# Second attention: the order k, first q, v; all of q's products in plain fp32; one instruction for a pair's offset

## The chip, the cores and the metric

One core of a Trainium2 chip runs the whole program in one launch. The metric is the device time of one execution in microseconds. TensorE (PE) does matmuls into PSUM; VectorE (DVE), ScalarE (ACT) and GpSimd (POOL) work on SBUF and PSUM; SyncE (SP) issues most DMA loads.

## The reference

Two blocks of a transformer on 256 tokens of width 1024, all in fp32. The first block has two layers, each attention and a convolutional FFN; the second block is a gated delta rule mixer with a mixture of experts. The change is in the second layer's attention:

```python
hk = rmsnorm(x, kv_norm)
k, v = jnp.split(hk @ w_kv_b, 2, axis=-1)            # 4 heads of 64 each
h = rmsnorm(x, attn_norm[l])
q = partial_rope(heads(h @ w_q_b[i], N_HEADS), cos, sin)   # 16 heads of 64
...
logits = jnp.einsum('bkgnqd,bknpd->bkgnqp', qb, kcat) * (HEAD_DIM ** -0.5)
logits = jnp.where(mask, logits, NEG)                # a window of 128
m = jnp.maximum(jnp.max(logits, axis=-1, keepdims=True), sink)
e = jnp.exp(logits - m)
p = e / (jnp.sum(e, axis=-1, keepdims=True) + jnp.exp(sink - m))
out = jnp.einsum('bkgnqp,bknpd->bkgnqd', p, vcat)
x = x + out.reshape(...) @ w_o
```

## The kernel before

Activations lie transposed, features on partitions: `x` is 8 blocks of 128 features by 256 tokens. A projection is done in chunks of 256 output columns: one DMA of 1 MB brings the chunk's weights (`raw`, 3 buffers), and each of the 8 feature blocks gives two products (the chunk's two column halves), each a 128x128 block of weights on 256 tokens, summed in PSUM (`acc`, 4 buffers).

A product comes in two forms. In the plain form the fp32 weights and the fp32 activations (`xf`) go to PE as they are (L262). In the split form both are cut into a high and a low part of type fp32r: ACT copies the high part (`whi`, L204; `xh`, L400), DVE subtracts to get the low one (`wlo`, L207; `xl`, L401), and PE does three matmuls, high by high, low by high, high by low (L217 to L219; in `proj_tm`, which gives v with tokens on partitions, L306 and L314 to L316). An `Act` holds activations with the first `plain` blocks in plain form and the rest split; in the second attention `plain` is 2 of 8, for `act` (k and v), `actq` (q) and `out`. Weights are split in pieces of 512 columns, 5 buffers of each part, so a chunk with 2 plain blocks has 3 pieces.

The second attention (its block begins at L770) goes: activations for k and v, row norms and tables for the rotation, activations for q, k's projection and rotation, v's projection, and then 4 chunks of q. A chunk holds two pairs of heads, each pair in `softmax_pair` and `attend_pair`: the mask is laid into PSUM by a matmul (L445), the scores are added (L447, L449), DVE takes the row maxima (`mm`, L451) and makes the offset `nb` (L457, L458), ACT does the exponentials with their sums (L463) and the sink's (L468), DVE scales (`pr`, L475), PE transposes (L489), DVE and ACT copy the transposed tiles to SBUF, and PE multiplies by v (L497). Then w_o in 4 chunks (first 2 blocks plain) and the FFN's w_up.

There is no order by hand here: the tile framework puts each engine's instructions in an order when the program is built, by readiness and by place in the program, so PE's queue mixes a pair's instructions with products of later chunks. Each engine then works through its own queue in that order. The block at the end of the program, for the experts, has its own scheduling and is not touched.

Of the kernel before, what the change touches and what calls it, by code (L numbers as in the profile page):

```python
# [13 lines left out]
F32 = mybir.dt.float32  # L14
F32R = mybir.dt.float32r
I32 = mybir.dt.int32
AF = mybir.ActivationFunctionType
ALU = mybir.AluOpType
# [3 lines left out]
P = 128  # L22
T = 256
D = 1024
KD = D // P
NH = 16
# [53 lines left out]
def tile_two_blocks(ctx: ExitStack, tc: tile.TileContext, A, out_ap):  # L80
    nc = tc.nc
# [3 lines left out]
    B = SimpleNamespace(few=2, n=0)  # L85
# [35 lines left out]
    x = cp.tile([P, KD, T], F32, name="x")  # L121
# [8 lines left out]
    sk = fp.tile([P, NH], F32, name="sk")  # L130
# [21 lines left out]
    masks = [fp.tile([P, 384], F32R, name=f"maskr{i}") for i in range(2)]  # L152
# [27 lines left out]
    class Act:  # L180


        def __init__(self, plain, n, tag=None, pool=None, bufs=2, sfx=""):
            pool = pool or B.wk
            self.plain = plain
            tags = ("xh", "xl") if tag is None else tag
            self.h = pool.tile([P, n, T], F32R, name="xh", tag=tags[0], bufs=bufs)
            self.l = pool.tile([P, n, T], F32R, name="xl", tag=tags[1], bufs=bufs)
            self.f = plain and pool.tile([P, plain, T], F32, name="xf", tag="xf" + sfx, bufs=bufs)
# [48 lines left out]
    def proj(*args, **kw):  # L238
        for _ in proj_steps(*args, **kw):
            pass  # L240
# [59 lines left out]
    def proj_tm(raw, act, evac, parts=None):  # L300

        pss = [B.pa.tile([P, T], F32, name="acc", tag="acc") for _ in range(2)]
        n = act.plain
        for t in range(2):
            for k in range(n):
                nc.tensor.matmul(pss[t], act.f[:, k, t * P : (t + 1) * P], raw[:, k * 256 : (k + 1) * 256], start=k == 0, stop=False)  # L306
        for a, n1, hi, lo in parts or parts_of(raw[:, n * 256 :], 2048 - n * 256, n * 256):
            hv = hi.rearrange("p (k c) -> p k c", c=256)
            lv = lo.rearrange("p (k c) -> p k c", c=256)
            for t in range(2):  # L310
                s = slice(t * P, (t + 1) * P)
                for k in range(n1 // 256):
                    kg = a // 256 + k
                    nc.tensor.matmul(pss[t], act.h[:, kg, s], hv[:, k, :], start=kg == 0, stop=False)  # L314
                    nc.tensor.matmul(pss[t], act.h[:, kg, s], lv[:, k, :], start=False, stop=False)
                    nc.tensor.matmul(pss[t], act.l[:, kg, s], hv[:, k, :], start=False, stop=kg == KD - 1)  # L316
        for t in range(2):
            evac(t, pss[t])
# [64 lines left out]
    def rstd_of(sums):  # L383
        return rstd_rows(rstd_cols(sums))

    def gained(src, gi):

        act = Act(2, KD)
        for _ in gained_steps(act.h, act.l, src, gi, act.f):
            pass  # L390
        return act

    def gained_steps(hi, lo, src, gi, full=None):
        for k in range(KD):
            g = nv[:, gi, k : k + 1]
            if full is not None and k < 2:
                nc.scalar.activation(full[:, k], src[:, k], AF.Copy, scale=g)
                continue
            h, l = (f(k) if callable(f) else f[:, k] for f in (hi, lo))
            nc.scalar.activation(h, src[:, k], AF.Copy, scale=g)  # L400
            nc.vector.scalar_tensor_tensor(l, src[:, k], g, h.bitcast(F32), op0=ALU.mult, op1=ALU.subtract)  # L401
            if k % 2:
                yield
# [21 lines left out]
    def rope_to(dst, ps, tab):  # L425

        raw = B.wk.tile([P, 2, T], F32, name="qraw", tag="qraw")
        sw = B.wk.tile([P, 2, T], F32, name="qsw", tag="qsw")
        nc.scalar.activation(raw, ps, AF.Copy)
        nc.vector.stream_shuffle(sw, raw, SWAP)  # L430
        nc.vector.tensor_tensor(dst, raw, tab[0], op=ALU.mult)
        nc.vector.tensor_tensor(sw, sw, tab[1], op=ALU.mult)
        nc.vector.tensor_tensor(dst, dst, sw, op=ALU.add)

    def softmax_pair(q, k, mask, sinks):

        cut = ((0, 128), (128, 384))
        mm = B.wk.tile([P, 2, 2], F32, name="mm", tag="mm")
        both = B.pb.tile([P, 2, 512], F32, name="sc", tag="sc", bufs=2)
        sc = [both[:, h, :384] for h in range(2)]  # L440
        hs = [slice(h * HD, (h + 1) * HD) for h in range(2)]

        edges = lambda x: x.rearrange("p (b c) -> p b c", c=P)[:, 0::2] if sinks is None else x
        for s in sc:
            nc.tensor.matmul(edges(s), identr, edges(mask), start=True, stop=False, skip_group_check=True)  # L445
        for s, h in zip(sc, hs):
            nc.tensor.matmul(s[:, 0:128], q[h, 0:128], k[h, 0:128], start=False, stop=True, skip_group_check=True)  # L447
        for s, h in zip(sc, hs):
            nc.tensor.matmul(s[:, 128:384], q[h, 128:256], k[h, :], start=False, stop=True, skip_group_check=True)  # L449
        for i, (a, b) in enumerate(cut):  # L450
            nc.vector.tensor_reduce(mm[:, :, i], both[:, :, a:b], axis=AX.X, op=ALU.max)  # L451
        nb = B.wk.tile([P, 2, 2], F32, name="nb", tag="nb")
        if sinks is None:
            nc.vector.tensor_scalar(nb, mm, -0.125, None, op0=ALU.mult)
        else:
            for h in range(2):
                nc.vector.tensor_scalar(nb[:, h], mm[:, h], 0.125, sinks[h], op0=ALU.mult, op1=ALU.max)  # L457
            nc.vector.tensor_scalar(nb, nb, -1.0, None, op0=ALU.mult)  # L458
        pr = B.wk.tile([P, 2, 384], F32, name="pr", tag="pr")
        sums = B.wk.tile([P, 2, 2], F32, name="sums", tag="sums")  # L460
        for h in range(2):
            for i, (a, b) in enumerate(cut):
                nc.scalar.activation(pr[:, h, a:b], sc[h][:, a:b], AF.Exp, bias=nb[:, h, i : i + 1], scale=0.125,  # L463
                                     accum_out=sums[:, h, i : i + 1])
        if sinks is not None:
            es = B.wk.tile([P, 2, 2], F32, name="es", tag="es")
            for h in range(2):
                nc.scalar.activation(es[:, h], nb[:, h], AF.Exp, bias=sinks[h], scale=1.0)  # L468
            nc.vector.tensor_tensor(sums, sums, es, op=ALU.add)
        rs = B.wk.tile([P, 2, 2], F32, name="rs", tag="rs")  # L470
        nc.vector.reciprocal(rs, sums)
        for h in range(2):
            for i, (a, b) in enumerate(cut):
                if sinks is not None or i:
                    nc.vector.tensor_scalar(pr[:, h, a:b], pr[:, h, a:b], rs[:, h, i : i + 1], None, op0=ALU.mult)  # L475
                else:
                    nc.scalar.activation(pr[:, h, a:b], pr[:, h, a:b], AF.Copy, scale=rs[:, h, i : i + 1])
        return pr, both
# [233 lines left out]
    with phase("ab", 4), tc.tile_pool(name="hp", bufs=1) as hp, weights("ab", 3, 5, 2048, 512):  # L712
# [6 lines left out]
        raw = B.wr.tile([P, 2048], F32, name="raw", tag="raw")  # L719
        for a in range(0, 2048, 512):  # L720
            nc.scalar.dma_start(raw[:, a : a + 512], A["w_v"][0][:, a : a + 512])
        act = Act(2, KD)
        ws = parts_of(raw[:, 512:], 1536, 512)
        both = []
# [14 lines left out]
        for c in range(4):  # L739
# [4 lines left out]
            if c == 1:  # L744
# [3 lines left out]
                y = rstd_cols(sums)  # L748
# [8 lines left out]
        for t in range(8):  # L757
            qk = B.wk.tile([P, 2, T], F32, name="qk", tag="qk")
            proj("w_qk", t, KD, act, None, both=lambda ps: rope_to(qk, ps, tab))
            pr, both = softmax_pair(qk[:, 0, :], qk[:, 1, :], masks[0], None)  # L760
# [7 lines left out]


        act = gained(x, 4)  # L770
        y = rstd_cols(sums)
        tab = tables(y)
        actq = gained(x, 1)
        k1, v1 = (hp.tile([P, 2, 256], F32, name=i, tag=t) for i, t in (("k1", "hh"), ("v1", "hl")))
        proj("w_kv", 0, KD, act, None, both=lambda ps: rope_to(k1, ps, tab))
        raw = B.wr.tile([P, 2048], F32, name="raw", tag="raw")
        nc.sync.dma_start(raw, A["w_kv"][1])
        proj_tm(raw, act, lambda t, ps: nc.scalar.activation(v1[:, t, :], ps, AF.Copy, scale=y[:, t : t + 1]))
        out = Act(2, KD)
        for c in range(4):  # L780
            q1 = B.wk.tile([P, 2, T], F32, name="q1", tag="qk")
            proj("w_q", c, KD, actq, None, both=lambda ps: rope_to(q1, ps, tab))
            for m in range(2):
                t = 2 * c + m
                kvp = t // 4
                heads = [4 * (2 * kvp + s) + t % 4 for s in range(2)]
                pr, both = softmax_pair(q1[:, m, :], k1[:, kvp, :], masks[1], [sk[:, h : h + 1] for h in heads])
                vs = [[v1[:, j, (2 * kvp + s) * HD : (2 * kvp + s + 1) * HD] for j in range(2)] for s in range(2)]
                attend_pair(pr, both, vs[0], vs[1], out, t)
        sums = Sums()  # L790
# [918 lines left out]
```

## Time and profile before

| | |
|---|---|
| time, median of 3 runs | 1313.37 us (1313.19 to 1313.55) |
| the profiled execution: time, span | 1312.89 us, 1311.1 us |
| busy: PE, weight loads, DVE, ACT | 98%, 88%, 78%, 60% |
| k's projection to the last pair's value products | about 324 to 399 us |

The span is the time from the first to the last instruction in the trace, and the rows' times count from its start. PE's matmuls are pipelined: what one costs in a run of them is read from the steps between starts, not from its duration. PEld is the loading of weights, which goes on beside matmuls. A row of the timeline that ends in x8 merges eight records.

### The profile page before, as it was taken

What the parts mean: (1) busy time and instruction counts of PE and PEld (TensorE: products, weight loads), DVE (VectorE), ACT (ScalarE), POOL (GpSimd) and SP (SyncE); (2) the same over time, 40 slices, a digit from 0 to 9 for tenths busy, and PEclk for the clock granted to TensorE, in tenths of its full rate; (3) what the DMA queues carried; (4) which work ended last, traced back from release to release, by engine and by line L of the source; (5) the groups of instructions that cost most, each with busy time, mean ns of one, the idle gap of its engine ahead of it and who ended that gap; (6) DMA issues with size and microseconds to landing.
All of it is one profiled execution on the core that took longest, in us unless ns stands there. A gap on an engine that the chain in (4) does not pass through costs nothing.

```text
span 1311.1 us, 26079 instructions
## 1 busy us (share of the span) xinstructions
PE 1278.9 (98%) x10092; PEld 1149.3 (88%) x10092; DVE 1019.1 (78%) x2215; ACT 790.2 (60%) x1628; POOL 28.5 (2%) x51
## 2 busy tenths in 40 slices
PE   7999999999999999999999999999999999999998
PEld 7888999999879999999888787888987888888877
DVE  6677989866788988755766888666368899999985
ACT  6555667755556677653434464644257887878763
POOL 1000000000000010000100000000000000000000
PEclk9999999999999999999999999999989999999999
DMA  7434555555423555662254323243437999999951
GB/s 285 143 101 139 180 187 176 177 190 177 156 97 130 173 193 184 225 215 79 97 152 126 100 60 102 66 134 99 170 130 288 360 340 354 365 358 376 347 192 35
DMA packets 69570, 244.50 MB, mean 186 GB/s; under 512 B 24128, under 2 KB 26176, under 8 KB 45632
## 3 DMA queue, kind: packets, MB, share of 16 engines
q1 hardware_dynamic: 68288, 241.26, 52.9%
q8 instruction: 81, 1.33, 0.4%
q10 hardware_dynamic: 1152, 1.51, 0.4%
q14 instruction: 49, 0.40, 0.1%
HBM read 240.12 MB, written 2.62 MB: 185 GB/s over the span
## 4 chain that ended last, share of the span: by engine, by line
PE 86%; DVE 9%; ACT 2%; issue 1%; DMA 1%; SPq 0%; DVEq 0%; ACTq 0%
PE acc L217 11%; PE acc L218 11%; PE acc L219 11%; PE acc L292 10%; PE gu L1351 4%; PE gu L1350 4%; PE gu L1352 4%; PE acc L262 4%; PE y L1379 2%; PE y L1380 2%; PE y L1381 2%; PE acc L1614 2%; PE o L1164 2%; DVE wlo L207 1%; PE sc L489 1%
## 5 line engine op out<-in xcount | busy, mean ns | idle before, releaser
L207 DVE TENSOR_TENSOR wlo<-raw,whi 128x512 fp32r<-128x512 f32 (+1 forms) x542 | 467.8, 878 | 102.4 <-ACT whi L204 98.2
L204 ACT ACTIVATE whi<-raw 128x512 fp32r<-128x512 f32 (+1 forms) x542 | 418.1, 780 | 191.9 <-PE acc L218 132.7
L217 PE MATMUL acc<-xh,whi 128*128 128x256 f32 x892 | 258.0, 290 | 0.0
L219 PE MATMUL acc<-xh,wlo 128*128 128x256 f32 x892 | 252.0, 283 | 0.0
L218 PE MATMUL acc<-xl,whi 128*128 128x256 f32 x892 | 251.0, 282 | 0.0
L219 PEld LDWEIGHTS acc<-xh,wlo 128*128 128x128 f32 x892 | 169.8, 190 | 2.5 <-issue 2.5
L217 PEld LDWEIGHTS acc<-xh,whi 128*128 128x128 f32 x892 | 167.7, 188 | 3.0 <-issue 1.5
L218 PEld LDWEIGHTS acc<-xl,whi 128*128 128x128 f32 x892 | 168.0, 188 | 2.5 <-issue 1.5
L292 PE MATMUL acc<-x,raw 128*128 128x256 f32 x640 | 154.0, 386 | 0.4 <-issue 0.4
L292 PEld LDWEIGHTS acc<-x,raw 128*128 128x128 f32 x640 | 116.4, 190 | 15.0 <-issue 0.8
L1351 PE MATMUL gu<-wlo,xgh 128*128 128x512 f32 x256 | 103.7, 405 | 0.0
L1352 PE MATMUL gu<-whi,xgl 128*128 128x512 f32 x256 | 101.0, 394 | 1.7 <-DVE xgl L1307 1.6
L1350 PE MATMUL gu<-whi,xgh 128*128 128x512 f32 x256 | 101.3, 396 | 0.0
L219 PE MATMUL acc<-hh,wlo 128*128 128x256 f32 x352 | 99.6, 283 | 0.0
L218 PE MATMUL acc<-hl,whi 128*128 128x256 f32 x352 | 99.6, 283 | 0.0
L217 PE MATMUL acc<-hh,whi 128*128 128x256 f32 x352 | 99.6, 283 | 0.0
L262 PE MATMUL acc<-xf,raw 128*128 128x256 f32 x296 | 71.3, 379 | 0.0
L217 PEld LDWEIGHTS acc<-hh,whi 128*128 128x128 f32 x352 | 67.6, 192 | 0.0
L219 PEld LDWEIGHTS acc<-hh,wlo 128*128 128x128 f32 x352 | 67.6, 192 | 0.0
L218 PEld LDWEIGHTS acc<-hl,whi 128*128 128x128 f32 x352 | 67.6, 192 | 0.0
L1352 PEld LDWEIGHTS gu<-whi,xgl 128*128 128x128 f32 x256 | 48.6, 190 | 12.2 <-DVE xgl L1307 3.4
L262 PEld LDWEIGHTS acc<-xf,raw 128*128 128x128 f32 x296 | 52.9, 190 | 5.6 <-issue 0.2
(423 smaller groups left out, 2290.4 us busy)
## 6 DMA issues: line engine op xcount, KB each, us to landing
raw<-w_gu SPq DMA_DIRECT2D x64, 1024.0 KB, 7.3
raw<-w_up SPq DMA_DIRECT2D x44, 1024.0 KB, 4.8
raw<-w_ed SPq DMA_DIRECT2D x32, 1024.0 KB, 7.2
raw<-w_gin SPq DMA_DIRECT2D x96, 256.0 KB, 3.3
raw<-w_down SPq DMA_DIRECT2D x16, 1024.0 KB, 4.9
raw<-w_qk SPq DMA_DIRECT2D x8, 1024.0 KB, 5.0
raw<-w_gout SPq DMA_DIRECT2D x32, 256.0 KB, 2.9
raw<-w_down SPq DMA_DIRECT2D x8, 768.0 KB, 4.3
```

The lines of the kernel that those rows point to most:

```text
L204: B.hi = nc.scalar.activation(hi[:, :m], raw[:, a : a + m], AF.Copy)
L207: i = eng.tensor_tensor(lo[:, :m], raw[:, a : a + m], hi[:, :m].bitcast(F32), op=ALU.subtract)
L217: nc.tensor.matmul(ps, wh, ah, start=first, stop=False, skip_group_check=True)
L218: nc.tensor.matmul(ps, wh, al, start=False, stop=False, skip_group_check=True)
L219: return nc.tensor.matmul(ps, wl, ah, start=False, stop=last, skip_group_check=True)
L262: nc.tensor.matmul(ps[:, m], rv[:, k, m * P : (m + 1) * P], full.f[:, k0 + k], start=k0 + k == 0 and m == 0, stop=k0 + k == nk - 1, skip_g ...
L292: nc.tensor.matmul(ps[:, m], raw[:, k, m * P : (m + 1) * P], act(k0 + k), start=k0 + k == 0 and m == 0, stop=k0 + k == nk - 1, skip_group_ ...
L1164: nc.tensor.matmul(o[:, t, h], at[:, d, blk], u[step][:, tu, h], start=i == 0, stop=i == 2)
L1350: nc.tensor.matmul(gu, xgh[:, kg, :], hv[:, k, :], start=kg == 0, stop=False)
L1351: nc.tensor.matmul(gu, xgh[:, kg, :], lv[:, k, :], start=False, stop=False)
L1352: nc.tensor.matmul(gu, xgl[:, kg, :], hv[:, k, :], start=False, stop=kg == KD - 1)
L1379: nc.tensor.matmul(y[g][c], hh[:, j, :], hi[:, s], start=first, stop=False)
```

## The change

Four edits, all in the second attention or in helpers that only it uses that way. q's activations become an `Act` of 8 plain blocks, which then takes one buffer of the high part's kind and none of the low part's. v's projection is called after q's first chunk instead of before it. The negated sinks are computed once (`less`), and a pair's offset becomes one instruction, min(-0.125 x max, -sink), where three made max(0.125 x max, sink) by head and then negated it. The first attention has no sinks and its offset stays as it is.

```diff
@@ class Act
+            if plain == n:
+                self.h = self.l = None
+                self.f = pool.tile([P, n, T], F32, name="xf", tag=tags[0], bufs=bufs)
+                return
@@ gained, gained_steps
-    def gained(src, gi):
-        act = Act(2, KD)
-        for _ in gained_steps(act.h, act.l, src, gi, act.f):
+    def gained(src, gi, plain=2):
+        act = Act(plain, KD)
+        for _ in gained_steps(act.h, act.l, src, gi, act.f, plain):
...
-            if full is not None and k < 2:
+            if full is not None and k < plain:
@@ softmax_pair
-            for h in range(2):
-                nc.vector.tensor_scalar(nb[:, h], mm[:, h], 0.125, sinks[h], op0=ALU.mult, op1=ALU.max)
-            nc.vector.tensor_scalar(nb, nb, -1.0, None, op0=ALU.mult)
+            nc.vector.scalar_tensor_tensor(nb, mm, -0.125, less, op0=ALU.mult, op1=ALU.min)
@@ the second attention
-        actq = gained(x, 1)
+        actq = gained(x, 1, KD)
+        less = B.wk.tile([P, NH], F32, name="less", bufs=1)
+        nc.vector.tensor_scalar(less, sk, -1.0, None, op0=ALU.mult)
         proj("w_kv", 0, KD, act, None, both=lambda ps: rope_to(k1, ps, tab))
-        raw = B.wr.tile([P, 2048], F32, name="raw", tag="raw")
-        nc.sync.dma_start(raw, A["w_kv"][1])
-        proj_tm(raw, act, lambda t, ps: nc.scalar.activation(v1[:, t, :], ps, AF.Copy, scale=y[:, t : t + 1]))
+        def values():
+            raw = B.wr.tile([P, 2048], F32, name="raw", tag="raw")
            nc.sync.dma_start(raw, A["w_kv"][1])
            proj_tm(raw, act, lambda t, ps: nc.scalar.activation(v1[:, t, :], ps, AF.Copy, scale=y[:, t : t + 1]))
         for c in range(4):
             q1 = B.wk.tile([P, 2, T], F32, name="q1", tag="qk")
             proj("w_q", c, KD, actq, None, both=lambda ps: rope_to(q1, ps, tab))
+            if not c:
+                values()
...
-                pr, both = softmax_pair(q1[:, m, :], k1[:, kvp, :], masks[1], [sk[:, h : h + 1] for h in heads])
+                pr, both = softmax_pair(q1[:, m, :], k1[:, kvp, :], masks[1], [sk[:, h : h + 1] for h in heads],
+                                        less[:, heads[0] : heads[1] + 1 : 4, None].to_broadcast([P, 2, 2]))
```

## Rows read from the trace of the kernel before

**Rows 1.** The page's busy time, share of the span and instructions by engine.

```profile
PE 1278.9 (98%) x10092; PEld 1149.3 (88%) x10092; DVE 1019.1 (78%) x2215; ACT 790.2 (60%) x1628; POOL 28.5 (2%) x51
```

**Rows 2.** Windows: length, then busy us of PE, PEld, DVE, ACT, POOL, clock.

```profile
338.00:354.00 16.00, 15.28 (x115) 13.98 (x113) 9.39 (x24) 7.30 (x22) 0.00 (x0) 1.00 0.38 132
354.00:370.00 16.00, 15.77 (x129) 13.41 (x130) 14.44 (x46) 11.54 (x40) 0.00 (x0) 1.00 0.35 120
370.00:386.00 16.00, 15.55 (x124) 12.42 (x124) 14.53 (x41) 8.73 (x30) 0.00 (x0) 1.00 0.23 79
386.00:399.00 13.00, 12.67 (x110) 10.19 (x109) 10.38 (x31) 7.40 (x28) 0.00 (x0) 1.00 0.27 89
```

**Rows 3.** Waits from 323.9 to 405 us: total us, times, longest.

```profile
ACT whi L204 <- PE acc L218: 10.4, 8, 2.7
...
PE sc L489 <- DVE pr L475: 1.5, 3, 0.8
```

**Rows 4.** Timeline of PE, a chunk of q: start us, us, instruction.

```profile
337.02 1.89 PE L262 MATMUL acc<-xf,raw 128*128 128x256 f32 x8
...
338.86 0.28 PE L218 MATMUL acc<-xl,whi 128*128 128x256 f32 x1
...
342.73 0.28 PE L219 MATMUL acc<-xh,wlo 128*128 128x256 f32 x1
```

**Rows 5.** Instructions by line and shape, 300 to 399 us, DVE and ACT.

```profile
L207 DVE TENSOR_TENSOR wlo<-raw,whi 128x512 fp32r<-128x512 f32 x40 | 27.3, 690 | 15.2 <-ACT whi L204 15.1
...
L401 DVE SCALAR_TENSOR_TENSOR xl<-x,nv,xh 128x256 fp32r<-128x256 f32 x8 | 3.7, 478 | 0.0
...
L457 DVE TENSOR_SCALAR nb<-mm,sk 128x2 f32<-128x2 f32 x16 | 2.9, 226 | 0.3
...
L458 DVE TENSOR_SCALAR nb<-nb 128x4 f32<-128x4 f32 x8 | 1.3, 168 | 0.2
...
L204 ACT ACTIVATE whi<-raw 128x512 fp32r<-128x512 f32 x40 | 25.2, 636 | 24.5 <-PE acc L218 19.6 <-PE acc L316 3.4 <-DVE wlo L207 1.5
```

**Rows 6.** Line L361, whole span: ns min, median, max.

```profile
L361 DVE SCALAR_TENSOR_TENSOR rs_y<-rs_t,rs_y x45: 147/161/169, 27.2 to 1286.4; 128x8 f32<-128x8 f32 x24, 128x2 f32<-128x2 f32 x21
```

**Rows 7.** Chain of waits, 340 to 400 us: first and last of three such pieces.

```profile
348.10 0.94 DVE mm L451 x2
...
388.18 1.03 DVE mm L451 x2
```

**Rows 8.** Timeline of ACT and PE behind the first pair's reduction.

```profile
349.91 1.28 ACT L463 ACT_TABLE_LOAD   x1 [2.53 <-DVE nb L458]
...
354.17 0.30 PE L489 MATMUL sc<-cst,pr 128*128 128x128 f32 x1 [0.82 <-DVE pr L475]
```

**Rows 9.** Timeline of PE where pairs and products mix.

```profile
354.42 0.38 PE L489 MATMUL sc<-cst,pr 128*128 128x128 f32 x2
...
370.98 0.49 PE L489 MATMUL sc<-cst,pr 128*128 128x128 f32 x3
...
372.90 0.45 PE L445 MATMUL sc<-maskr,identr 128*128 128x384 f32 x1
...
393.95 0.60 PE L262 MATMUL acc<-xf,raw 128*128 128x256 f32 x2
...
396.00 0.88 PE L497 MATMUL sc<-pts,v 128*64 128x128 f32 x12
396.81 0.55 PE L489 MATMUL sc<-cst,pr 128*128 128x128 f32 x3
```

**Rows 10.** The loads of w_kv: us from issue to landing.

```profile
DMA to landing us min/median/max: 4.9/5.5/6.1
```

**Rows 11.** Timeline of PE: v begins, first scores, first value products.

```profile
330.58 0.60 PE L306 MATMUL acc<-raw,xf 128*128 128x256 f32 x2
...
346.88 0.38 PE L447 MATMUL sc<-k,q 64*128 64x128 f32 x2
...
356.98 0.33 PE L497 MATMUL sc<-pts,v 128*64 128x128 f32 x2
```

More of the change, by code (lines that the diff above doesn't have):

```diff
@@ L384, in rstd_of, with gained_steps @@
         return rstd_rows(rstd_cols(sums))
-    def gained(src, gi):
-        act = Act(2, KD)
-        for _ in gained_steps(act.h, act.l, src, gi, act.f):
+    def gained(src, gi, plain=2):
+        act = Act(plain, KD)
+        for _ in gained_steps(act.h, act.l, src, gi, act.f, plain):
             pass
         return act
-    def gained_steps(hi, lo, src, gi, full=None):
+    def gained_steps(hi, lo, src, gi, full=None, plain=2):
         for k in range(KD):
             g = nv[:, gi, k : k + 1]
-            if full is not None and k < 2:
+            if full is not None and k < plain:
                 nc.scalar.activation(full[:, k], src[:, k], AF.Copy, scale=g)
@@ L433, in rope_to, with softmax_pair @@
         nc.vector.tensor_tensor(dst, dst, sw, op=ALU.add)
-    def softmax_pair(q, k, mask, sinks):
+    def softmax_pair(q, k, mask, sinks, less=None):
         cut = ((0, 128), (128, 384))
@@ L772, in tile_two_blocks @@
         tab = tables(y)
-        actq = gained(x, 1)
+        actq = gained(x, 1, KD)
         k1, v1 = (hp.tile([P, 2, 256], F32, name=i, tag=t) for i, t in (("k1", "hh"), ("v1", "hl")))
+        less = B.wk.tile([P, NH], F32, name="less", bufs=1)
+        nc.vector.tensor_scalar(less, sk, -1.0, None, op0=ALU.mult)
         proj("w_kv", 0, KD, act, None, both=lambda ps: rope_to(k1, ps, tab))
-        raw = B.wr.tile([P, 2048], F32, name="raw", tag="raw")
-        nc.sync.dma_start(raw, A["w_kv"][1])
-        proj_tm(raw, act, lambda t, ps: nc.scalar.activation(v1[:, t, :], ps, AF.Copy, scale=y[:, t : t + 1]))
+        def values():
+            raw = B.wr.tile([P, 2048], F32, name="raw", tag="raw")
+            nc.sync.dma_start(raw, A["w_kv"][1])
+            proj_tm(raw, act, lambda t, ps: nc.scalar.activation(v1[:, t, :], ps, AF.Copy, scale=y[:, t : t + 1]))
         out = Act(2, KD)
```

## The prediction

> **What bounds the kernel now.** I read the page's busy shares first [rows 1]: PE is busy 98% of the span, DVE 78%, ACT 60%. A busy PE is not yet a PE at its peak, so I then cut the stage that changes into stretches [rows 2]. From 338 to 399 us PE's busy column is short by only 0.72, 0.23, 0.45 and 0.33 us in the four stretches; the clock is 1.00 throughout. DVE, though, is at 14.4 of 16 us in the two middle stretches. The reader should see two things: PE has almost no holes, and DVE is the next engine in line.
>
> The waits [rows 3] say which holes there are. Only three of some size stop PE: the transposes of a pair (L489) wait for DVE's scaling of `pr` (L475), 1.5 us together, 0.8 the longest. The larger waits in the list are ACT and DVE waiting for PE, or for each other with PE at work. So in this stage the time is PE's instructions plus about 1.5 us of waits plus what PE loses where it changes from one kind of matmul to another.
>
> **The price of a product.** A product here is one 128x128 weight block on 256 columns. The chunk of q at 337 us shows both forms [rows 4]. Four plain products are 8 records, 1.89 us from first start to last end, one record 0.379: (1.89 - 0.379) / 7 = 0.216 us a record, two records a product, 0.432 us. The 12 split products behind them are 36 records; from the second (338.86) to the last (342.73) are 34 steps, 0.114 us each, three records a product, 0.342 us. A plain product costs PE 0.090 us more than a split one.
>
> The change makes 6 of 8 blocks plain, for 2 column halves and 4 chunks: 48 products, 48 x 0.090 = **+4.3 us** of PE, on the engine that sets the time.
>
> The Trainium skill (FP8 and Floating Point Precision, TensorE Precision Notes) says that true fp32 takes four passes through the array where reduced precision takes one, a rule that speaks against this change. By that page, as an estimate, a plain product would be four times the 0.114 us of a split record, 0.455 us, and the term 48 x 0.114 = 5.5 us; the trace has 0.432 us, so the measurement decides and 4.3 us stands.
>
> **What goes from DVE and ACT** [rows 5]. A chunk of q was split in three pieces of 512 columns: 12 pieces, 12 x 0.690 = 8.3 us of DVE (L207) and 12 x 0.636 = 7.6 us of ACT (L204). Six low halves of the activations (L401) go, 6 x 0.478 = 2.9 us of DVE; their ACT copies stay, as plain copies. A pair's offset was 2 x 0.226 + 0.168 = 0.62 us in three instructions; as one scalar_tensor_tensor on 128x4 it is not in the trace. The nearest row is the same operation on 128x8 or 128x2, 0.147 to 0.169 us [rows 6]; the other end is L457's 0.226, which also reads sinks. I take 0.16, so 0.46 a pair, 3.7 us for 8 pairs. The new `less` is one instruction of about 0.17 us, long before it is read. DVE loses 14.7 us in all, ACT 7.6 us. This is off PE's path: it pays only where PE waits for these engines.
>
> **What of it reaches the path.** The chain of waits goes over from PE to DVE's reduction three times in this stage, first at 348.10 and last at 388.18 us [rows 7]. Behind the first one come the offset, a table load of 1.28 us, the exponentials, sums and scaling, and PE's transpose starts at 354.17 after 0.82 us of wait [rows 8]. The change takes 0.46 us out of that chain and empties the queues around it. But PE's order is fixed when the program is built and is drawn up anew with the change, so a transpose may again stand a little too early in its queue. Of the 1.5 us I take half: **-0.75 us**, ends 0 and -1.5.
>
> Changing between kinds of matmul costs PE something. With split products as filler, 370.98 to 372.90 us holds three transposes, five split records and the 12 records of the value products [rows 9]: 1.92 us, where 3 x 0.11 + 5 x 0.114 + 0.81 = 1.71. With plain records as filler, 393.95 to 396.81 holds six transposes, six plain records and 12 value records: 2.86 us, where 6 x 0.11 + 6 x 0.216 + 0.81 = 2.77. (A transpose adds 0.49 - 0.38 = 0.11, from groups of three and two; 0.81 is the distance from 396.00 to 396.81.) So plain filler loses 0.1 us less each time. Six pairs have q's products as filler: **-0.6 us**, ends 0 and -1.3 (twice a pair).
>
> **The moved step.** v's projection, with its DMA, moves behind the first chunk of q. On SP its 1 MB issue changes places with the next one, q's first; such loads land in 5 to 6 us [rows 10], before PE reaches them: q's first chunk now follows k's projection, which ends at 330.58, and v's follows 32 x 0.216 = 6.9 us later, near 337.5 [rows 11]. On PE v's products, 8 plain records and 36 split ones, 8 x 0.216 + 36 x 0.114 = 5.8 us, now cover the rotation of q's first chunk, which took 4.0 us from the last product (342.84, where the masks begin) to the first score (346.88) [rows 11]. Before, masks and q's second chunk covered it. If that cover were gone it would cost those 4.0 us, and on ACT and DVE only k's and v's own splits stand ahead of that rotation. v itself is what is late next: it would be out near 344 us, and the first value product stood at 356.98 us [rows 11]. I cost the move at nothing, on both sides. A raw buffer of q is now held until PE's last product instead of until the last split. The first chunk would give its buffer up near 337.5 us, the third chunk's data would land near 342.5, and PE wants it after v and the second chunk (5.8 + 6.9 us), near 350: covered by some 7 us.
>
> New waits from the redrawn order: 0, ends 0 and +2.0 us (a table load of 1.28 plus a split of 0.64 queued ahead of a pair).
>
> **Sum.** 4.3 - 0.75 - 0.6 + 0 = +3.0 us. The profiled execution has 1312.89 us, its span 1311.1; that becomes 1315.9. The median of the three runs lies 0.48 us higher, at 1313.37, so the forecast is **1316.4 us**. The ends are 4.3 - 1.5 - 1.3 = +1.5 and 4.3 + 2.0 = +6.3.
>
> **Rivals.** A difference of 0.2% is 2.6 us, about what a measurement of this kernel can tell from no change.
>
> *The cover holds everything.* All waits at the transposes vanish and changing kinds loses twice what I took: +1.5 us, 1314.9 us. For it: the shorter chain and an emptier DVE stand exactly in front of the three waits. Against it: the other pairs also wait a little, and nothing says the new order is better placed. 0.38.
>
> *DVE and ACT set the stage's pace (faster).* The chain does run through the reduction and the exponentials three times [rows 7]. If PE only seems full, taking 14.7 us from DVE lets the whole stage shrink. PE's weight loads leave 2.0 + 2.6 + 3.6 + 2.8 = 11.0 us unfilled between 338 and 399 us [rows 2]. All of it gone would be 4.3 - 11.0 = -6.7 us, 1306.7 us; it ends below the 0.2% only once 6.9 of the 11.0 us are recovered. Against it: those stretches hold the score and value products, whose weight loads are short, and PE's true waits are 1.5 us. 0.07.
>
> The Trainium skill (Perfetto Trace Analysis, Identifying the Most-Contended Engine) says that matmul busy time misjudges PE's headroom and that the share of weight loads tells it better. By that rule this rival would be the forecast; the trace agrees only in part, since the steps between records leave no such holes.
>
> *A new wait.* In the new order a pair's transposes stand ahead of q's next plain products while ACT is still behind a table load and v's splits, and none of the old waits goes: 4.3 - 0.6 + 2.0 = +5.7 us, 1319.1 us. It leaves my forecast's own range once the waits cost 2.1 us more than in my sum. For it: the first pair's 0.82 us of that kind. Against: there is more filler than before. 0.10.
>
> My forecast has 0.45. **Chances:** slower by over 0.2% 0.45 + 0.10 = 0.55, within 0.38, faster 0.07. The range leaves out about 1 in 10 on each side: below, the faster case and the deepest of the cover; above, the new wait at its full price: 1313.2 to 1318.6 us. The forecast case alone spans 1316.0 to 1318.5.
>
> **What the new profile would show.** Per chunk of q 32 plain records at 0.216 us, no whi and wlo pieces of `w_q` (12 of each fewer); DVE's busy time down about 15 us, ACT's about 8, PE's up; one offset instruction of about 0.16 us a pair; the first score near 342 us instead of 346.88; no waits of PE for a DMA. I would be wrong if PE's waits for `pr` grew or vanished with more than 1.5 us, if a plain product cost other than 0.432 us next to transposes, or if the stages behind, whose instructions don't change, were ordered differently and moved by microseconds.

## The result, and the profile after

The changed kernel takes 1319.96 us (median of 5 runs, 1318.99 to 1321.96), beside 1313.19 for the kernel before on the same chip: a ratio of 1.0065, interval 1.0045 to 1.0084. It is slower, as forecast, but by 6.8 us where the forecast had 3.0, and above the range's end of 1318.6. The profiled execution took 1319.96 us with a span of 1318.3.

The page of the changed kernel, busy time by engine:

```profile
PE 1286.3 (98%) x10044; PEld 1154.3 (88%) x10044; DVE 1007.6 (76%) x2182; ACT 787.4 (60%) x1616; POOL 26.4 (2%) x51
```

Against [rows 1] PE has 48 records fewer and is busy 7.4 us longer; DVE lost 11.5 us and ACT 2.8. To see where the time came, I cut both traces at the same instructions: the row norms' matmuls that end a layer's part, the first and the last of the experts' matmuls. Windows of the kernel before, in order: first attention with its w_o, first FFN, second attention with its w_o, second FFN, delta rule, routing, experts. Columns as in [rows 2].

```profile
21.46:135.34 113.88, 113.28 (x867) 100.59 (x865) 84.55 (x195) 65.46 (x173) 5.49 (x2) 1.00 0.39 135
135.34:326.76 191.42, 191.26 (x1562) 189.28 (x1561) 156.73 (x323) 125.23 (x242) 0.00 (x0) 1.00 0.53 182
326.76:414.31 87.55, 85.83 (x674) 75.42 (x673) 70.67 (x196) 50.91 (x151) 0.00 (x0) 1.00 0.35 121
414.31:605.07 190.76, 189.94 (x1551) 187.79 (x1551) 150.32 (x308) 119.50 (x229) 5.70 (x6) 1.00 0.53 183
605.07:961.47 356.40, 346.09 (x3769) 302.32 (x3769) 241.89 (x737) 157.12 (x466) 14.65 (x35) 1.00 0.38 117
961.47:981.96 20.49, 18.62 (x95) 16.65 (x95) 13.70 (x50) 15.23 (x21) 0.00 (x0) 0.75 0.10 29
981.96:1265.86 283.90, 281.30 (x1312) 231.77 (x1310) 263.12 (x321) 225.90 (x282) 0.00 (x0) 0.99 0.93 346
```

The same windows of the changed kernel:

```profile
22.27:137.05 114.78, 114.41 (x867) 101.94 (x865) 83.80 (x192) 65.77 (x173) 5.19 (x2) 1.00 0.39 132
137.05:331.15 194.10, 193.77 (x1562) 191.74 (x1562) 155.31 (x319) 126.82 (x242) 0.00 (x0) 1.00 0.53 180
331.15:422.77 91.62, 90.08 (x623) 75.34 (x624) 60.48 (x166) 44.85 (x139) 0.00 (x0) 1.00 0.33 114
422.77:615.88 193.11, 192.31 (x1551) 190.18 (x1550) 150.32 (x308) 120.89 (x229) 3.98 (x6) 1.00 0.53 180
615.88:972.31 356.43, 345.86 (x3769) 302.19 (x3769) 241.78 (x737) 157.51 (x466) 14.66 (x35) 1.00 0.39 117
972.31:990.69 18.38, 15.83 (x94) 14.36 (x95) 15.70 (x57) 15.41 (x22) 0.00 (x0) 0.91 0.22 76
990.69:1272.64 281.95, 280.80 (x1312) 231.95 (x1310) 261.27 (x313) 225.39 (x281) 0.00 (x0) 0.99 0.93 346
```

The stage that changes grew by 4.07 us (87.55 to 91.62). But three stages whose matmuls are the same in number and form grew too: the first attention by 0.90, the FFNs by 2.68 and 2.35, at a clock of 1.00 in both traces and with PE busy nearly throughout. The first attention runs ahead of every changed instruction, and so does the first FFN but for its end, where q's activations begin (DVE has four instructions fewer there). Routing and experts gave 2.11 and 1.95 back.

What grew there is the single step, the time from one matmul's start to the next one's. PE's timeline of the kernel before in the first FFN, split products on the feature activations:

```profile
160.19 0.28 PE L217 MATMUL acc<-xh,whi 128*128 128x256 f32 x1
...
160.90 0.28 PE L217 MATMUL acc<-xh,whi 128*128 128x256 f32 x1
```

The same loop in the changed kernel (its L221 is L217 of before):

```profile
164.77 0.29 PE L221 MATMUL acc<-xh,whi 128*128 128x256 f32 x1
...
165.49 0.29 PE L221 MATMUL acc<-xh,whi 128*128 128x256 f32 x1
```

Six steps take 0.71 us in the one, 0.118 each, and 0.72 us in the other, 0.120 each. Two digits hardly show it; the mean of the steps below 0.14 us between two split records of 256 columns on feature activations does: 117.0 ns in 2,497 steps before, 119.7 ns in 2,398 after (85 and 66 longer ones are left out). 2.7 ns by 2,400 steps is 6.5 us.

In the changed stage, PE's timeline shows q's first chunk, v's plain products, and the first mask and scores:

```profile
335.90 7.07 PE L266 MATMUL acc<-xf,raw 128*128 128x256 f32 x32
342.81 1.89 PE L310 MATMUL acc<-raw,xf 128*128 128x256 f32 x8
348.86 0.51 PE L449 MATMUL sc<-maskr,identr 128*128 128x384 f32 x2
349.30 0.49 PE L451 MATMUL sc<-k,q 64*128 64x128 f32 x4
```

DVE's timeline there, the end of q's rotation, the row maxima with what they waited for, and the new offset:

```profile
345.57 0.69 DVE L437 TENSOR_TENSOR q<-q,qsw 128x512 f32<-128x512 f32 x1
350.27 1.02 DVE L455 TENSOR_REDUCE mm<-sc 128x2 f32<-128x256 f32 x2 [4.01 <-PE sc L453]
351.33 0.16 DVE L461 SCALAR_TENSOR_TENSOR nb<-mm,less 128x4 f32<-128x4 f32 x1
```

And PE's waits from 327 to 407 us:

```profile
PE sc L492 <- DVE pr L478: 1.1, 3, 0.5
PE rstd L371 <- DVE rs_y L365: 0.4, 1, 0.4
PE st L349 <- DVE acc_sq L336: 0.2, 1, 0.2
```

The reader should see that within the stage the forecast's picture holds: 32 plain records a chunk, no wait for a DMA, short waits for `pr`, PE full.

**What could reach back in time.** Only the layout. `less` holds 16 floats, 64 bytes in each partition. It is taken from a pool that lies ahead of the FFN's hidden activations (`hh`, `hl`; k and v use their tiles), the raw weights and the cut weights (`whi`, `wlo`), so all of these lie 64 bytes further on in the whole first block. The feature activations (`xh`, `xl`) lie ahead of it and stay. Places in the program's memory plan, modulo 128 bytes, and the mean step (steps below 0.14 us between two split records of 256 columns, by what the first one streams):

| kernel | features, hidden, weights at | features to weights | step | hidden to weights | step |
|---|---|---|---|---|---|
| before | 96, 32, 32 | 64 | 117.0 ns | 0 | 120.0 ns |
| changed | 96, 96, 96 | 0 | 119.7 ns | 0 | 120.0 ns |

So my theory after the result: a split step depends on where moving data and weights lie to each other, and `less` moved them level. The rival: the new order of instructions, or the instruction itself, slows the program.

### The profile page after: what moved, and what is told of

It reads as the page before. It is cut to its first block, busy times and chain, and to the rows that moved or that the text cites. A ratio compares the mean times of both kernels' runs of the same rounds, so it can differ in the third digit from the quotient of the medians.

```text
span 1318.3 us, 25922 instructions
## 1 busy us (share of the span) xinstructions
PE 1286.3 (98%) x10044; PEld 1154.3 (88%) x10044; DVE 1007.6 (76%) x2182; ACT 787.4 (60%) x1616; POOL 26.4 (2%) x51
## 4 chain that ended last, share of the span: by engine, by line
PE 86%; DVE 9%; ACT 2%; issue 1%; DMA 1%; SPq 0%; DVEq 0%; ACTq 0%
PE acc L222 11%; PE acc L223 11%; PE acc L221 11%; PE acc L296 10%; PE acc L266 5%; PE gu L1362 4%; PE gu L1361 4%; PE gu L1363 4%; PE y L1390 2%; PE y L1391 2%; PE y L1392 2%; PE acc L1625 2%; PE o L1175 2%; PE sc L492 1%; DVE wlo L211 1%
## 5 line engine op out<-in xcount | busy, mean ns | idle before, releaser
L211 DVE TENSOR_TENSOR wlo<-raw,whi 128x512 fp32r<-128x512 f32 (+1 forms) x530 | 460.1, 882 | 108.5 <-ACT whi L208 105.5
L221 PE MATMUL acc<-xh,whi 128*128 128x256 f32 x844 | 245.3, 291 | 0.0
L223 PE MATMUL acc<-xh,wlo 128*128 128x256 f32 x844 | 241.4, 286 | 0.0
L222 PE MATMUL acc<-xl,whi 128*128 128x256 f32 x844 | 240.1, 285 | 0.0
L223 PEld LDWEIGHTS acc<-xh,wlo 128*128 128x128 f32 x844 | 159.8, 189 | 2.2 <-issue 2.2
L221 PEld LDWEIGHTS acc<-xh,whi 128*128 128x128 f32 x844 | 160.1, 190 | 1.6 <-issue 0.3
L222 PEld LDWEIGHTS acc<-xl,whi 128*128 128x128 f32 x844 | 159.5, 189 | 2.2 <-issue 1.4
L221 PE MATMUL acc<-hh,whi 128*128 128x256 f32 x352 | 99.6, 283 | 0.0
L266 PE MATMUL acc<-xf,raw 128*128 128x256 f32 x392 | 94.8, 381 | 0.0
L266 PEld LDWEIGHTS acc<-xf,raw 128*128 128x128 f32 x392 | 70.5, 190 | 8.7 <-issue 1.5
L221 PEld LDWEIGHTS acc<-hh,whi 128*128 128x128 f32 x352 | 67.6, 192 | 0.0
L1361 PEld LDWEIGHTS gu<-whi,xgh 128*128 128x128 f32 x256 | 48.3, 189 | 10.5
```

The costliest lines, as they stand in the source:

```text
L211: i = eng.tensor_tensor(lo[:, :m], raw[:, a : a + m], hi[:, :m].bitcast(F32), op=ALU.subtract)
L221: nc.tensor.matmul(ps, wh, ah, start=first, stop=False, skip_group_check=True)
L222: nc.tensor.matmul(ps, wh, al, start=False, stop=False, skip_group_check=True)
L223: return nc.tensor.matmul(ps, wl, ah, start=False, stop=last, skip_group_check=True)
L266: nc.tensor.matmul(ps[:, m], rv[:, k, m * P : (m + 1) * P], full.f[:, k0 + k], start=k0 + k == 0 and m == 0, stop=k0 + k == nk - 1, skip_g ...
L1361: nc.tensor.matmul(gu, xgh[:, kg, :], hv[:, k, :], start=kg == 0, stop=False)
```

## The experiments

Each was timed in 5 rounds beside the kernel before, on one chip for each group of four; a ratio is to the kernel before beside it. In what follows "the stage" is the second attention with its w_o, "the FFNs" are the first and the second FFN's windows, and feature and hidden steps are the mean steps of the table above.

**The shift alone.** The kernel before with a larger `es`, the last tile of that pool. The order of instructions is the same.

```diff
-            es = B.wk.tile([P, 2, 2], F32, name="es", tag="es")
+            es = B.wk.tile([P, 2, 6], F32, name="es", tag="es")[:, :, 0:2]
```

> The kernel before, its instructions and their order unchanged; only the tile of the sinks' exponentials is padded, so that everything allocated behind it in this phase (the FFN's hidden tiles, the raw weights, the weight pieces) lies 64 bytes further on, as the 64 bytes of the negated sinks make it lie in the changed kernel. Theory A, placement: the split products' steps in projections from the activations' tiles go from 0.117 to 0.120 us, some 2,500 steps, +6.5 us (5 to 8). Theory B, the change's own instructions and the order drawn up anew: 0 us. Theory C, a difference between executions only: 0 us, and steps that vary from run to run.

Measured: 1318.98 us, ratio 1.0051 (1.0034 to 1.0069). Windows of this run, first attention to second FFN:

```profile
22.59:137.41 114.82, 114.44 (x866) 101.90 (x865) 83.50 (x191) 65.82 (x173) 5.19 (x2) 1.00 0.39 131
137.41:331.12 193.71, 193.60 (x1562) 191.67 (x1561) 156.94 (x323) 126.77 (x242) 0.00 (x0) 1.00 0.53 180
331.12:419.43 88.31, 86.80 (x673) 76.41 (x673) 70.82 (x196) 50.97 (x151) 0.00 (x0) 1.00 0.35 120
419.43:612.49 193.06, 192.26 (x1551) 190.13 (x1550) 150.55 (x308) 120.97 (x229) 5.71 (x6) 1.00 0.53 180
```

64 unused bytes make the program 0.5% slower. The four stages grow by 0.94, 2.29, 0.76 and 2.30 us, 6.3 together; feature steps are at 119.7 ns. The order cannot be the cause, since it is the same.

**The change with 64 more bytes**, by the same edit of `es`: all later tiles lie 128 bytes further, level with their old places modulo 128.

```diff
@@ in the changed kernel
-            es = B.wk.tile([P, 2, 2], F32, name="es", tag="es")
+            es = B.wk.tile([P, 2, 6], F32, name="es", tag="es")[:, :, 0:2]
```

> The changed kernel with 64 bytes more of padding behind the negated sinks, 128 in all, its instructions and their order unchanged. Theory A, that two operands 64 bytes apart modulo 128 are read faster than two that are 0 apart: the steps return to 0.117 us and the time falls by 6 to 7 us against the changed kernel, to +1 to +4 us over the kernel before. Theory A2, that any shift costs: as slow as the changed kernel or slower. Theory B: no difference from the changed kernel, +6.8 us.

Measured: 1315.26 us, ratio 1.0031 (1.0012 to 1.0050); feature steps 117.7 ns, FFNs 192.08 and 191.05 us, the stage 91.62 as in the changed kernel. Half of the loss goes when another 64 bytes are given away. What stays is 0.31% or 4.1 us. By the windows the stage is 4.07 us longer than before, but the FFNs, too, are still 0.66 and 0.29 longer: 128 bytes don't quite restore the old step.

**The offset alone**, which brings `less` and its 64 bytes:

```diff
-            for h in range(2):
-                nc.vector.tensor_scalar(nb[:, h], mm[:, h], 0.125, sinks[h], op0=ALU.mult, op1=ALU.max)
-            nc.vector.tensor_scalar(nb, nb, -1.0, None, op0=ALU.mult)
+            nc.vector.scalar_tensor_tensor(nb, mm, -0.125, less, op0=ALU.mult, op1=ALU.min)
```

> Of the change only the negated sinks and the pair's offset in one instruction; q in split form, v before q. The 64 bytes of the negated sinks are in it. Theory A: +5 to +7 us (the shift's 6.5, less up to 1 us of shorter waits). Theory B: 0 to -1 us.

Measured: 1319.62 us, ratio 1.0061 (1.0038 to 1.0084); feature steps 119.7 ns, FFNs 193.76 and 193.07 us. An edit that saves DVE two instructions a pair costs about as much as the whole change, 8.0 us by the ratio, a little over the 5 to 7 that I expected of the place.

**The offset with 64 more bytes**, in the order of instructions of the run just told:

```diff
@@ in the kernel with the offset alone
-            es = B.wk.tile([P, 2, 2], F32, name="es", tag="es")
+            es = B.wk.tile([P, 2, 6], F32, name="es", tag="es")[:, :, 0:2]
```

> The offset in one instruction with the negated sinks, and another 64 bytes behind them, so that all tiles allocated later lie 128 bytes further in place of 64; the order of instructions is that of the run with the offset alone. Theory that the place modulo 128 made that run slow: split steps back at 117 ns, first attention at 113.9 and the FFNs at 191.4 and 190.8 us as before; the whole within 1 us of before (1311 to 1312), the remainder being the second attention's 0.7 us from a changed order. Rival that the instruction with negated sinks, or the order drawn up with it, costs the 7 us: 1317 to 1319 again.

Measured: 1314.17 us, ratio 1.0016 (1.0001 to 1.0030); feature steps 117.6 ns, FFNs 191.70 and 191.04. With the order unchanged, the place takes 5 us off (1319.62 to 1314.17). The stage is 88.74, 1.2 us more than before: the offset gains nothing there. The whole is 2.1 us over before by the ratio, where I had at most 1; the FFNs are 0.28 us longer each.

**Plain q alone** (with the helpers it needs; v first, old offset, no tile moved):

```diff
-        actq = gained(x, 1)
+        actq = gained(x, 1, KD)
```

> Of the change only q's plain products; the old offset in three instructions, v before q, no tile more and so nothing shifted. Theory A: the plain products' price alone, 48 x 0.090 = 4.3 us less about 1 us at changes of kind and waits, +2.5 to +4.5 us, split steps at 0.117 us. Theory B: most of the 6.8 us, +5 us or more.

Measured: 1317.31 us, ratio 1.0039 (1.0022 to 1.0056). Windows of this run, first FFN to second FFN:

```profile
137.04:328.46 191.42, 191.26 (x1562) 189.28 (x1561) 155.38 (x319) 125.22 (x242) 0.00 (x0) 1.00 0.53 182
328.46:421.09 92.63, 89.99 (x626) 75.61 (x625) 63.33 (x182) 44.51 (x139) 0.00 (x0) 1.00 0.33 114
421.09:611.86 190.77, 189.95 (x1551) 187.81 (x1550) 150.24 (x308) 119.33 (x229) 4.28 (x6) 1.00 0.54 183
```

The FFNs are those of before to 0.01 us, so these windows can be read to small fractions, and of the three the stage alone grows, by 5.1 us. The rest of this trace is not so good a measure: at 1322.52 us it was the slowest of the 12 executions, with the lowest mean granted clock, 0.989. In its delta rule, 360.04 us beside 356.40, two stretches of 3.4 and 6.9 us ran at a granted clock of 0.50 and 0.51, the level of 1.2 GHz (PE had been busy for 7.7 of the 10 us ahead of the first and 5.5 of the 6.8 ahead of the second); before, it was one of 3.5 us. Freeing DVE of 7.3 us and ACT of 6.4 us in the stage gave PE nothing. By the ratio, too, it is 5.1 us, more than the 2.5 to 4.5 of the view of place and price and as much as the other view asked; but feature steps are at 117.3 ns, so the excess lies in the stage and not in slower steps.

**The order alone**: the kernel before with v's projection called after q's first chunk.

```diff
+            if not c:
+                values()
```

> The kernel before with v's projection called after q's first chunk, and nothing else: q's products stay split in 6 of 8 blocks, the offset stays three instructions, no tile moves. The prediction's view, in which the order is worth nothing by itself: second attention with w_o at 87.5 to 88 us, as before (87.55), whole program within 0.5 us of before. View of additive parts: the changed kernel was +3.3 us in that stage net of its layout, plain q alone +5.1, the offset alone +0.7, so the order is worth about -2.5 us: stage at 85 us, program at 0.998 of before. View that the order is of use only beside plain q (whose chunk leaves DVE and ACT with nothing to cut while v's pieces are made): stage at 88 us or above here.

Measured: 1313.58 us, ratio 1.0015 (0.9999 to 1.0031); the stage 88.70 us. I had expected -2.5 us if the parts add; it is +1.15, so they don't, and the view of use only beside plain q fits. PE's waits for `pr` are 2.3 us here, 1.5 before.

**Plain q with the order** (old offset, no tile moved):

```diff
@@ in the changed kernel
-            nc.vector.scalar_tensor_tensor(nb, mm, -0.125, less, op0=ALU.mult, op1=ALU.min)
+            for h in range(2):
+                nc.vector.tensor_scalar(nb[:, h], mm[:, h], 0.125, sinks[h], op0=ALU.mult, op1=ALU.max)
+            nc.vector.tensor_scalar(nb, nb, -1.0, None, op0=ALU.mult)
```

> The changed kernel with the old offset (three instructions, no negated sinks, so no tile moves from where it lay before): plain q and the moved projection of v. The stage (second attention with w_o; before 87.55, changed kernel 91.62, plain q alone 92.63, order alone 88.71). View that the moved v pays beside plain q: 91.6 or less, as in the changed kernel, the whole at 1315 to 1316. View that the order pays nothing there either and the offset's instruction is what takes 1 us off: 92.6 or more, the whole at 1316 to 1317. Steps of split products outside the stage at 117 ns in either view, first attention and FFNs as before.

Measured: 1315.29 us, ratio 1.0020 (1.0005 to 1.0034); the stage 91.62 us, exactly the changed kernel's, 1.0 less than with plain q alone. The order is what takes that 1 us off. PE's waits with plain q alone show where it may lie:

```profile
PE sc L449 <- DVE xl L218: 1.1, 1, 1.1
```

One pair's mask waited 1.1 us for DVE there, and no mask waits with the order.

**Plain q with the offset**, v first, 128 bytes of shift:

```diff
@@ in the changed kernel with 64 more bytes
-            if not c:
-                values()
@@ ahead of the loop over q's chunks
+        proj_tm(raw, act, lambda t, ps: nc.scalar.activation(v1[:, t, :], ps, AF.Copy, scale=y[:, t : t + 1]))
```

> Plain q and the offset in one instruction, v's projection in its old place ahead of q, with 128 bytes of shift so that the weights keep their place modulo 128. View that the offset's instruction takes 1 us off plain q: stage at 91.6. View that it does nothing by itself (as alone, where the stage was 1.2 us longer): 92.6 to 93.8. The whole at 1315.5 to 1318.

Measured: 1317.09 us, ratio 1.0042 (1.0025 to 1.0058); the stage 92.19 us, between the two views: the offset takes off 0.4 us at most.

**Weights apart from both.** The step on hidden activations was 120.0 ns in every kernel so far, at a difference of 0. Here, in the kernel before, `es` is larger as above and k's tile, which shares its place with `hh`, is 64 bytes longer.

```diff
-        k1, v1 = (hp.tile([P, 2, 256], F32, name=i, tag=t) for i, t in (("k1", "hh"), ("v1", "hl")))
+        k1, v1 = (hp.tile([P, 2, n], F32, name=i, tag=t)[:, :, 0:256] for i, t, n in (("k1", "hh", 2824), ("v1", "hl", 256)))
```

> The kernel before with two tiles made larger and nothing else (the same instructions in the same order): the cut weights lie 64 bytes apart, modulo 128, from the FFN's hidden activations as well as from the feature activations, where before they are apart from the latter and level with the former. Theory that only the place decides: the 1,054 steps on hidden activations fall from 120 to about 117 ns, the feature ones stay at 117, each FFN is 1.6 us shorter (189.8 and 189.2 us), and the program about 3 us (1308, 0.9977 of before). Rival that the hidden steps are slow for another reason (their tiles' size or what DVE and ACT do beside them): they stay at 120 ns and the time is that of before. Rival that any larger tile costs time: 1316 or more.

Measured: 1308.35 us, ratio 0.9978 (0.9962 to 0.9993), faster than both kernels. PE's timeline in the first FFN's second product, before:

```profile
300.23 0.28 PE L217 MATMUL acc<-hh,whi 128*128 128x256 f32 x1
...
302.03 0.28 PE L217 MATMUL acc<-hh,whi 128*128 128x256 f32 x1
```

and with the weights apart:

```profile
300.18 0.28 PE L217 MATMUL acc<-hh,whi 128*128 128x256 f32 x1
...
302.00 0.28 PE L218 MATMUL acc<-hl,whi 128*128 128x256 f32 x1
```

15 steps take 1.80 us in the one (0.120) and 16 take 1.82 us in the other (0.114). Over all 1,054 such steps the mean fell from 120.0 to 113.3 ns, more than the 117 that I expected. The run also tells the difference of places from either place: the hidden activations lie at 96 modulo 128 here and with the shift alone, the weights at 32 here and in the kernel before, and in both of those the hidden step is 120.0. Its windows, first FFN to second FFN:

```profile
135.51:323.69 188.18, 187.91 (x1561) 185.95 (x1561) 156.75 (x323) 125.12 (x242) 0.00 (x0) 1.00 0.55 185
323.69:411.61 87.92, 86.31 (x673) 75.95 (x673) 70.76 (x196) 50.90 (x151) 0.00 (x0) 1.00 0.35 121
411.61:599.16 187.55, 186.73 (x1552) 184.61 (x1551) 150.44 (x308) 119.50 (x229) 5.70 (x6) 1.00 0.54 186
```

The FFNs are 3.24 and 3.21 us shorter; the first attention (114.48 us) and the stage are 0.60 and 0.37 longer, so 5.5 us are gained by these windows. The ratio shows 2.9 us of them (at most 5.0, by the interval), the two medians 3.9; the profiled execution, at 1305.25 us, was the fastest of the 12. Where the rest goes in other executions isn't shown. Executions of one kernel differ by more than that, and the granted clock goes with it: of the 30 of the kernel before beside the first four runs, those with a mean granted clock of 0.997 took 1304.49 to 1308.88 us and those with 0.992 took 1312.86 to 1315.39.

**32 bytes.** The kernel before with k's tile 32 bytes longer (2820 in place of 2824, `es` as it was): differences of 32 and 96.

```diff
-        k1, v1 = (hp.tile([P, 2, 256], F32, name=i, tag=t) for i, t in (("k1", "hh"), ("v1", "hl")))
+        k1, v1 = (hp.tile([P, 2, n], F32, name=i, tag=t)[:, :, 0:256] for i, t, n in (("k1", "hh", 2820), ("v1", "hl", 256)))
```

> The kernel before, same instructions in the same order, with one tile 32 bytes longer: the cut weights then lie 32 bytes from the feature activations and 96 from the hidden ones, modulo 128 (before: 64 and 0). If any difference other than 0 serves: feature steps stay at 117 ns, hidden ones fall from 120 to about 113 (as they did at 64), the FFNs at 188.2 and 187.6 us, the whole at 1306 to 1308. If only 64 serves (the two halves of 128 bytes): feature steps rise to 120 and hidden ones stay, the whole at 1318, as with the shift of 64. If 32 and 96 are in between: 1310 to 1314.

Measured: 1313.76 us, ratio 1.0013 (1.0002 to 1.0025); feature steps 118.6 ns, hidden 118.3, the FFNs 191.60 and 191.02 us. In between on both sides: what counts is how far apart the two lie, not only whether they are level.

**The whole change in the best layout** (k's tile as for the weights apart; `less` gives the other 64 bytes):

```diff
@@ in the changed kernel
-        k1, v1 = (hp.tile([P, 2, 256], F32, name=i, tag=t) for i, t in (("k1", "hh"), ("v1", "hl")))
+        k1, v1 = (hp.tile([P, 2, n], F32, name=i, tag=t)[:, :, 0:256] for i, t, n in (("k1", "hh", 2824), ("v1", "hl", 256)))
```

> All of the change, with the tile of k enlarged as in the best layout: weights 64 bytes from both kinds of activations. Theory of two parts that add, the change's own +4 us in the second attention and the layout's -6.5 us by the trace (-4 by the medians of the unchanged program with this layout): stage at 91.6, FFNs at 188.2 and 187.6, the whole 4 us over the best layout without the change, that is 1309 to 1313 beside 1312 for before. Rival that the change costs elsewhere too: 1314 or above.

Measured: 1309.49 us, ratio 0.9991 (0.9977 to 1.0005); the stage 91.34 us, the FFNs 189.06 and 187.54. By the spans (1306.5 and 1303.5) the change costs 3.0 us in this layout too, by the ratios (0.9991 and 0.9978, on two chips) 1.7.

**Order and offset in the best layout, q left split:**

```diff
@@ in the changed kernel with that tile
-        actq = gained(x, 1, KD)
+        actq = gained(x, 1)
```

> The moved projection of v and the offset in one instruction, q left split, with the layout in which the weights are 64 bytes apart from both kinds of activations. If the parts add: layout -3 us, order -2.5, offset 0 to +0.7, so 1306 us (0.996 of before), the fastest of all. If the order is of no use without plain q: 1308.5 (the layout alone). If the layout is not what made the shifts: 1312 or above.

Measured: 1309.07 us, ratio 0.9981 (0.9968 to 0.9994); the stage 88.06 us. It is the layout's gain and nothing more: the stage is 0.14 us longer than in the best layout alone.

## Why the prediction missed

**The failed step: `less` was costed as "one instruction of about 0.17 us".** Its time was right in kind; its 64 bytes had no term at all, and the sum was made on the premise that stages whose instructions don't change keep their time. I had named that premise as what would make me wrong, but for the order of instructions; what broke it was the place of the data. Missing term: 6.3 us by the windows of the run with the shift alone, 4.5 us by the ratios of the changed kernel with and without 64 more bytes (1.0065 less 1.0031). With those bytes the change gives +4.1 us beside my +3.0, and 1316.4, which is 1.0024 of 1313.19, lies inside that run's interval (1.0012 to 1.0050). The rival of a new wait had 1319.1 us, close to the 1319.96 measured; that is chance, since the waits that it was about became shorter.

**The price of plain q: right, a little high.** A plain record took (7.07 - 0.379) / 31 = 0.216 us, as forecast. The split record of my chunk, 0.114, was a quick one: the mean of the feature steps in the stage before is 115.8 ns (258 steps), which makes 48 x (0.432 - 0.347) = +4.1 us in place of +4.3.

**The gains on the path: not there.** The waits for `pr` went from 1.5 us to 1.1 in the changed kernel, 1.4 both in the changed kernel with 64 more bytes and in the run of plain q with the order, where I took 0.75 off. The 0.6 us for changing kinds was read from two stretches of 2 to 3 us and doesn't appear: 4.1 - 0.1 leaves +4.0, and the stage grew by 4.07 in the run of plain q with the order, where no tile moved.

**DVE and ACT: off the path, as argued.** Added up row by row, the instructions that went and came take 14.6 us off DVE and 7.2 off ACT (I had 14.7 and 7.6); the stage's busy columns, where overlapping instructions count once, fell by 10.2 and 6.1. PE's time grew by what its products cost. The rival in which they set the pace has fallen: plain q alone relieves both and adds 5.1 us. One argument that I held against it was half wrong: only the weight loads of transposes and value products are short (139 and 136 ns), those of the scores take 185 to 188, as long as a split product's 189. By the Trainium skill (Perfetto Trace Analysis, Identifying the Most-Contended Engine) the share of weight loads would tell PE's headroom; the fastest and the slowest of the kernels here, by median, have the same, 1143.7 of 1303.5 us and 1154.3 of 1318.3, 88%. It doesn't tell them apart.

**The move of v: small, and wrong in place.** I costed it at nothing and expected the first score near 342 us. It stood at 349.30, 18.2 us after the stage's start where before it was 20.1: q's rotation was done at 346.26, but in PE's queue the masks and scores stood behind all of v's products. That left no hole in PE; beside plain q the order is worth -1.0 us in the stage, beside split q +1.15. PE waited for no load, though ACT did, 3.4 us for a chunk of w_o and 1.5 us for v's weights.

**The rest.** That routing and experts are 4 us shorter after is no part of this. Before, routing ran at a granted clock of 0.75, after at 0.91 (windows above), and its length was 17.7 to 20.5 us over all 14 traces. The experts' 282 us appear in the four kernels with plain q and v moved, and in one without either; their cause I leave open.

**What stays open.** That the difference of places sets the step is shown: the same instructions in the same order in three layouts, in both directions, with a value in between. Why is not. The two reads of one memory getting in each other's way would fit, but no run separates that, and the raw weights, which ACT and DVE read, move with the cut ones in every run. Nor is it shown why steps on hidden activations reach 113 ns at 64 bytes while those on features stay at 117. That 128 is the right period rests on the 128-byte shifts, and they don't bring back quite the same step: the feature steps are 117.6 to 117.7 in the six kernels with one, 117.0 to 117.3 in the four in which nothing moved. Modulo 512 the features lie 192 bytes past the weights in those four, 64 in the six and 128 in the slow ones, and the hidden activations at 113 ns lie 448 past them, so a longer period isn't excluded.

## What to carry to other kernels

A small new tile is not free because it is small: where PE is full, look at what lies behind it in memory, and ahead of any other reading compare the steps of a loop that the change did not touch. If that has moved, pad the tile and measure again before judging the edit. And the reverse is a gain to be had: in this kernel, 64 bytes between weights and moving data, modulo 128, gave 0.2% without an instruction changed, where no part of the change gained anything over the kernel before.

## What the runs showed of the hardware

PE's step between split products (fp32r, 128x128 weights, 256 columns of activations) depends on the difference of the places of moving data and weights within a partition; counted modulo 128 bytes, at 0 it is 119.7 to 120.0 ns, at 32 and 96 118.3 to 118.6, at 64 113.3 (hidden activations) and 117.0 to 117.7 (features). The granted clock was 1.00 in these loops. Plain fp32 records kept their 0.216 us in the changed layout. The Trainium skill (SBUF — State Buffer, SBUF: two separate sides) says that PE never waits on anyone at its ports, and the same page (A bandwidth-pool intuition that's wrong (but worth ruling out)) that weight loads have an independent read port of their own. The runs here don't contradict the ports, but the step is not independent of where the two reads lie: 6.7 ns of 120 between level and apart on the hidden activations. The measurement decides.
